# Forward decayed keys turned by VectorE and a round trip through HBM, instead of by TensorE

## The chip, the cores and the metric

The kernel runs on one core of one Trainium2 chip. The metric is the device time of one execution in microseconds, the median over runs; lower is better. The profile names the engines: PE is TensorE (matmul) and PEld its weight loads, DVE is VectorE, ACT is ScalarE, POOL is GpSimd, and SP is SyncE, which issues nearly all DMAs here.

## The reference, cut to what matters

One layer of an encoder over 1024 tokens of width 1024: an RMS norm, one input projection, two branches (bidirectional gated linear attention, and a pooling mixer), a gated merge, and a SwiGLU feed-forward. All is float32. The change touches the attention alone, 4 heads with keys of 128 and values of 256 features, once forward and once backward in time:

```python
b = jnp.cumsum(log_a, axis=3)            # decay within a chunk, per key feature
q_e = q * jnp.exp(b)
k_e = k * jnp.exp(-b)
k_d = k * jnp.exp(b_last - b)
scores = jnp.einsum('bhncd,bhnsd->bhncs', q_e, k_e)     # masked afterwards
o_intra = jnp.einsum('bhncs,bhnse->bhnce', scores, v)
kv = jnp.einsum('bhnsd,bhnse->bhnde', k_d, v)           # sums over the tokens of a chunk
# state: S_n+1 = diag(decay_n) S_n + kv_n
o_inter = jnp.einsum('bhncd,bhnde->bhnce', q_e, s_in)
```

The scores sum over key features, so they want the decayed keys with the features on partitions. The product `kv` sums over tokens, so it wants the same keys with the tokens on partitions.

## The kernel before, in words

Every float32 operand of a large product is split into a high part in TensorE's fast float32 form (a cast on ACT) and the low remainder (a subtract on VectorE or POOL); a product is three matmuls, high by high, high by low and low by high (`products`, L270). `split_to` (L199) is that cast and subtract.

The program is written out in order by hand: each engine executes its own instructions in the order in which the program lists them, and waits only for what its next instruction needs. `pump` (L161) is called after each group of three matmuls of a main stage (projections) and starts pieces of side work between them: a generator yields how many such groups pass before it goes on. `attention(h)` is such a generator. While head h is worked on, the main stage is a projection: values and then queries and keys of later heads, and for the last head the output gate `r`.

A head works on 8 chunks of 128 tokens, in two halves of 512 tokens, with d = 0 for the forward and d = 1 for the backward direction; a key tile is called by (half, d). In this order: the decays of the four (half, d), each a prefix scan on VectorE (`decay`), exponentials on ACT, and `apply_decay`, which makes the decayed keys `ke` on VectorE and the decayed queries `qe` on POOL. `transposed_keys` (L896) turns one `ke` tile token-major: four 128x128 transposes on TensorE into one bank of PSUM (`kp`), then `split_to` into a tile `kt`. The backward tiles (1,1) and (0,1) are turned before the backward scan over the chunks n = 7 down to 1. A step of a scan is `advance` (L904): three matmuls into a bank `kv`, an update of the state `st` on VectorE, and two scaled copies on ACT, one that goes to the output products (`sb` backward, `sf` forward) and one that the next step reads (`so`). During the step n = 7 the last `apply_decay`, of (1,0), is issued. After the step n = 3 the forward tile (0,0) is turned. Then come the scores of the first half (`scores`: matmuls into two banks `sc`, a masked merge on VectorE, and a cast and a subtract into `p`), a pause of six groups, and the forward loop over n = 0 to 7 (products of `p` and `v`, of `qe` and the states, into a bank `op`). After its step n = 0 the forward tile (1,0) is turned; the scores of the second half follow its step n = 1.

Work tiles of 4 KB per partition come from one ring of 39 buffers (`slot`, L97): raw weights, sums, keys, queries, values, states. A new tile is handed the buffer that has been free longest, in the program's order, and its first writer waits for that buffer's last reader. PSUM has 8 banks, 3 for the projections and 5 for the attention (`ps_g`). SP's queue carries the loads of weights (`raw`, L208), of sums (`wsum`, L597), of head outputs (`ol`, L1033), and the stores of sums and heads, each in program order; SP can be far ahead of the other engines, as it waits only for buffers and data.

Of the kernel before, what the change touches and what calls it, by code (L numbers as in the profile page):

```python
# [10 lines left out]
F32 = mybir.dt.float32  # L11
F32R = mybir.dt.float32r
# [5 lines left out]
P = 128  # L18
# [4 lines left out]
HALF = 512  # L23
HEADS = 4
# [5 lines left out]
GROUPS = 4  # L30
WINDOWS = (2, 4, 8, 16)
PAD = 8
D_FF = 2816
FT = D_FF // P
EPS = 1e-6
# [18 lines left out]
def kernel(  # L54
# [20 lines left out]
    nc = tc.nc  # L75
# [12 lines left out]
    dram = ctx.enter_context(tc.tile_pool(name="dram", bufs=1, space=bass.MemoryType.DRAM))  # L88
# [4 lines left out]
    def name(s):  # L93
        count[0] += 1
        return f"{s}_{count[0]}"

    def slot(dtype=F32, shape=(2, HALF), s="slot"):  # L97
        return slots.tile([P, *shape], dtype, tag="slot", name=name(s))

    def t2(width=HALF, dtype=F32, s="t"):  # L100
        return tmp.tile([P, width], dtype, tag="t2", name=name(s), padded_shape=[P, HALF + 2 * PAD])

# [3 lines left out]
    def vec(width, s="v"):  # L106
        return small.tile([P, width], F32, tag="vec", name=name(s), bufs=12)

    def bank(pool, s="ps"):
        return pool.tile([P, HALF], F32, tag=pool.name, name=name(s))  # L110

    def as_f32(ap):
        return ap.bitcast(F32)
# [4 lines left out]

    keepf = tmp.tile([P, HALF], F32, tag="t2", name="keepf", padded_shape=[P, HALF + 2 * PAD])
    nc.gpsimd.memset(keepf[:, :P], 1.0)  # L120
# [12 lines left out]

    edge = const.tile([P, 2, GROUPS, PAD], F32, tag="edge", name="edge")
    nc.gpsimd.memset(edge[:, :, :, :], 1.0)
    for g, w in enumerate(WINDOWS):
        for i in range(w // 2):
            nc.gpsimd.memset(edge[:, 0, g, i : i + 1], w / (i + w // 2))
        for i in range(1, w // 2):
            nc.gpsimd.memset(edge[:, 1, g, PAD - i : PAD - i + 1], w / (i + w // 2))  # L140

# [57 lines left out]
    def split_to(hi, lo, src, eng=nc.vector):  # L199
        nc.scalar.copy(hi, src)  # L200
        eng.tensor_tensor(lo, src, as_f32(hi), op=ALU.subtract)  # L201
# [392 lines left out]
    def loading(srcs, tiles):  # L594
        def loads():
            for t, src in zip(tiles, srcs):
                nc.sync.dma_start(t, src)  # L597

        yield loads, None, None
        for _ in range(2):  # L600
            yield None, None, None
# [23 lines left out]
    def unit_jobs(n):  # L625
        raw = [slot(F32, (KT, P), "fraw")[:, :, :] for _ in range(2)]
        a11, a12, a21, a22 = (t[:, 4 * j : 4 * j + 4, :].rearrange("p k c -> p (k c)") for t in raw for j in range(2))
        yield from loading(
            [w_ffn_in[:, c0 : c0 + P].rearrange("(k p) c -> p k c", p=P) for c0 in (f_order[n] * P, D_FF + f_order[n] * P)], raw
        )  # L630
# [100 lines left out]
            aside.pop(0)  # L731


    o_heads, unscaled = {}, []
    HOLD, SCORES = 5.0, 6

# [76 lines left out]
    def attention(h):  # L813


        qe, ke = {}, {}
# [48 lines left out]
        def exponentials(half, d):  # L865
            if half not in qe:
                qe[half] = slot(s="qe")
            cs, tot, e_q = zs[half, d], totals[half, d], qe[half]
            f = vec(12, "fac")
            sign = INV_NORMALIZER if d == 0 else -INV_NORMALIZER  # L870
            nc.scalar.activation(e_q[:, d, :], cs[:, :], AF.Exp, scale=sign)
            nc.scalar.activation(cs[:, :], cs[:, :], AF.Exp, scale=-sign)
            nc.scalar.activation(f[:, :8], tot[:, :], AF.Exp, scale=INV_NORMALIZER)
            fac[half, d] = f

        def apply_decay(half, d):
            if half not in ke:
                ke[half] = slot(s="ke")
            f, e_q, e_k = fac[half, d], qe[half], ke[half]
            f2 = f[:, :8].rearrange("p (n a) -> p n a", a=2)  # L880
            nc.vector.tensor_tensor(e_k[:, d, :], zs[half, d][:, :], k[:, half, :], op=ALU.mult)
            nc.gpsimd.tensor_tensor(e_q[:, d, :], e_q[:, d, :], q[:, half, :], op=ALU.mult)
            nc.gpsimd.tensor_tensor(f[:, 8:], f2[:, :, 0], f2[:, :, 1], op=ALU.mult)
# [9 lines left out]
        def chunk_of(e, n, d):  # L893
            return e[n // 4][:, d, (n % 4) * CH : (n % 4 + 1) * CH]

        def transposed_keys(half, d):  # L896
            kp = bank(ps_g, "kp")
            for i in range(4):
                nc.tensor.transpose(kp[:, i * P : (i + 1) * P], chunk_of(ke, 4 * half + i, d), ident[:, :])
            kt = slot(F32R, s="kt")  # L900
            split_to(kt[:, 0, :], kt[:, 1, :], kp[:, :])
            return kt

        def advance(old, n, d, kt, dst, ends=False):  # L904

            kv = bank(ps_g, "kv")
            products(kv[:, :DV], tokens((kt[:, 0, :], kt[:, 1, :]), n), value(n))
            new = s1((DV,), "st")[:, :]
            after = factor(n, d, "after")
            if old is None:  # L910
                nc.vector.tensor_scalar(new, kv[:, :DV], after, None, op0=ALU.mult)
            else:
                nc.vector.scalar_tensor_tensor(
                    new, kv[:, :DV], after, old[:, :], op0=ALU.mult, op1=ALU.add
                )
            following = n + 1 if d == 0 else n - 1
            nc.scalar.activation(dst, new, AF.Copy, scale=factor(following, d, "before"))
            if ends:
                return None
            old = s1((DV,), "so")  # L920
            nc.scalar.activation(old[:, :], new, AF.Copy, scale=factor(following, d, "whole"))
            return old

        def scores(half):
            sc = [bank(ps_g, "sc") for _ in range(2)]
            for d in range(2):
                for i in range(4):
                    n = 4 * half + i
                    nc.tensor.matmul(
                        sc[d][:, i * CH : (i + 1) * CH], chunk_of(ke, n, d), chunk_of(qe, n, d),  # L930
                        start=True, stop=True,
                    )
            hi, lo = (t2(dtype=F32R, s="p")[:, :] for _ in range(2))
            nc.vector.copy_predicated(sc[1][:, :], keep.rearrange("p n c -> p (n c)"), sc[0][:, :])
            split_to(hi, lo, sc[1][:, :])
            return hi, lo
# [17 lines left out]
        kts = {(1, 1): transposed_keys(1, 1)}  # L954
# [2 lines left out]
        decay(1, 0)  # L957
        yield HOLD - 2
        kts[0, 1] = transposed_keys(0, 1)
        exponentials(1, 0)  # L960
        yield 2.5
        def value(n):
# [4 lines left out]
        for n in range(NT - 1, 0, -1):  # L967
            m = n - 1
            while n not in v_tiles[h]:
                yield 0.5  # L970
            old = advance(old, n, 1, kts[n // 4, 1], sb[m // 4][:, m % 4, :], m == 0)
            if n == 7:
                apply_decay(1, 0)
            yield 1.2
            if n == 3:
                kts[0, 0] = transposed_keys(0, 0)
                yield 0.5
        p = scores(0)
        yield SCORES
# [5 lines left out]
        for n in range(NT):  # L985
            half, i = n // 4, n % 4
            op = bank(ps_g, "op")
            products(op[:, :DV], tokens(p, n), value(n), last=False)
            terms = []
            if n < NT - 1:  # L990
                terms.append((chunk_of(qe, n, 1), sb[half][:, i, :]))
            if n > 0:
                terms.append((chunk_of(qe, n, 0), sf[:, :]))
            for j, (a, b) in enumerate(terms):
                if j == len(terms) - 1 and n < NT - 1:
                    sf = s1((DV,), "sf")
                    old = advance(old, n, 0, kts[half, 0], sf[:, :], n == NT - 2)
                nc.tensor.matmul(op[:, :DV], a, b, start=False, stop=j == len(terms) - 1)
            nc.vector.tensor_copy(o[half][:, i, :], op[:, :DV])
            nc.scalar.activation(  # L1000
                op[:, DV:], op[:, :DV], AF.Square, scale=1.0 / 16.0, accum_out=ms[:, n : n + 1]
            )
            if n == 0:
                yield 0.38
                kts[1, 0] = transposed_keys(1, 0)
            if n == 1:
                yield 0.75
                q_next = scores(1)
            if n == 3:
                p = q_next  # L1010
            yield 1.02
# [236 lines left out]
    def pooled(g, u, hi, lo):  # L1248
        width = WINDOWS[g]
        n = HALF + 2 * PAD  # L1250
        for half in range(2):
# [4 lines left out]
            while 2 * step < width:  # L1256
# [6 lines left out]
                s, step = a, 2 * step  # L1263
            e = slice(PAD, 2 * PAD) if half == 0 else slice(HALF, PAD + HALF)
            nc.vector.tensor_tensor(s[:, e], s[:, e], edge[:, half, g, :], op=ALU.mult)
# [404 lines left out]

    units = [ReadyUnit(n) if n < READY else Unit(w_ffn_in, (f * P, D_FF + f * P)) for n, f in enumerate(f_order)]

# [391 lines left out]
    for at, p in enumerate(OUT_ORDER):  # L2064
# [9 lines left out]
        for i in range(CLOSE if closing else n_of):  # L2074
            n = at * n_of + i
# [57 lines left out]
```

## Time and profile before

| what | value |
|---|---|
| median of 3 runs | 1374.98 us (1374.72 to 1375.22) |
| profiled execution, first to last instruction | 1373.4 us |
| PE busy | 1361.4 us, 99% |
| PEld busy | 1132.9 us, 82% |
| DVE, ACT, POOL busy | 836.8, 647.3, 752.1 us |
| DMA | 251.97 MB, mean 183 GB/s |
| the four heads' attention | about 85 to 325 us of the span |

The profile gives the first-to-last span of the profiled execution; the time of a run lies 1.6 us above it at the median. In the rows that follow, a group of instructions is told as engine, line, operation, output<-inputs, count, busy time and mean duration in ns. In rows in order of time the first two numbers are start and duration in us; square brackets give the idle time of the engine just before, and what ended it. Rows of equal kind that stand together are merged (x4).

### The profile page before, as it was taken

To read this page: it belongs to the slowest core of one execution; us is meant where nothing else is said; L and a number is where in the kernel's file an instruction comes from. 1 tells how busy PE (TensorE), PEld (TensorE's weight loads), DVE (VectorE), ACT (ScalarE), POOL (GpSimd) and SP (SyncE) were. 2 spreads that over 40 slices of the span, in tenths; PEclk is the share of its full clock that TensorE was granted. 3 is DMA by queue.
4 is the path that set the end of the run, shared out by engine and by line. 5 is a ranking of instruction groups with operands and counts; after the bars stand their busy time and mean duration, and the time that the engine had idled before them with its cause. 6 is when DMAs were issued, how large, how long until landed. Compare 5 with 4: busy or idle time off the path is not lost. (4 is left out here: it accounts for less than half of the span.)

```text
span 1373.4 us, 17879 instructions
## 1 busy us (share of the span) xinstructions
PE 1361.4 (99%) x6310; PEld 1132.9 (82%) x6310; DVE 836.8 (61%) x1034; ACT 647.3 (47%) x1177; POOL 752.1 (55%) x557
## 2 busy tenths in 40 slices
PE   9999999999999999999999999999999999999998
PEld 7888888888888888888888888888888888888886
DVE  6974556554735777678883955655566556343375
ACT  7365666755534445554346533333333334444253
POOL 3323723222597547667764376666676667455454
PEclk9999999999999999999999999999999999999999
DMA  6321523314778569995416355555544447985451
GB/s 227 113 87 52 181 90 92 95 60 123 245 236 278 186 198 308 373 386 216 150 71 241 112 174 176 176 176 177 176 145 137 146 136 266 384 301 187 169 215 77
DMA packets 167834, 251.97 MB, mean 183 GB/s; under 512 B 11160, under 2 KB 94144, under 8 KB 167744
## 3 DMA queue, kind: packets, MB, share of 16 engines
q1 hardware_dynamic: 167600, 250.57, 53.8%
q8 instruction: 49, 0.80, 0.2%
q14 instruction: 41, 0.34, 0.1%
q10 hardware_dynamic: 144, 0.26, 0.0%
HBM read 168.74 MB, written 82.05 MB: 183 GB/s over the span
## 5 line engine op out<-in xcount | busy, mean ns | idle before, releaser
L201 POOL TENSOR_TENSOR wl<-fs,wh 128x512 fp32r<-128x512 f32 x124 | 173.1, 1400 | 163.5 <-ACT wh L200 104.0
L273 PE MATMUL ps<-gh,wh 128*128 128x512 f32 x616 | 240.5, 390 | 0.0
L273 PE MATMUL ps<-gl,wh 128*128 128x512 f32 x616 | 239.8, 389 | 0.3 <-DVE gl L1691 0.3
L273 PE MATMUL ps<-gh,wl 128*128 128x512 f32 x616 | 239.7, 389 | 0.0
L201 POOL TENSOR_TENSOR wl<-fraw,wh 128x512 fp32r<-128x512 f32 x93 | 134.0, 1442 | 75.0 <-ACT wh L200 72.4
L201 POOL TENSOR_TENSOR ol<-gor,oh 128x1024 fp32r<-128x1024 f32 (+1 forms) x42 | 101.3, 2417 | 86.0 <-ACT oh L200 71.7
L273 PE MATMUL ps<-hh,wh 128*128 128x512 f32 x356 | 145.1, 408 | 0.7 <-ACT ga L1474 0.7
L273 PE MATMUL ps<-hh,wl 128*128 128x512 f32 x356 | 139.0, 390 | 0.0
L273 PE MATMUL ps<-hl,wh 128*128 128x512 f32 x356 | 138.8, 390 | 0.0
L273 PEld LDWEIGHTS ps<-gl,wh 128*128 128x128 f32 x616 | 115.7, 188 | 24.5 <-DVE gl L1691 0.7
L273 PEld LDWEIGHTS ps<-gh,wh 128*128 128x128 f32 x616 | 115.7, 188 | 24.1 <-ACT hb L1710 0.2
L273 PEld LDWEIGHTS ps<-gh,wl 128*128 128x128 f32 x616 | 115.7, 188 | 23.9
L273 PE MATMUL ps<-oh,oh 128*128 128x512 f32 x308 | 119.8, 389 | 0.0
L273 PE MATMUL ps<-ol,oh 128*128 128x512 f32 x308 | 119.8, 389 | 0.0
L273 PE MATMUL ps<-oh,ol 128*128 128x512 f32 x308 | 119.8, 389 | 0.0
L201 POOL TENSOR_TENSOR wl<-wraw,wh 128x512 fp32r<-128x512 f32 x56 | 92.3, 1679 | 44.7 <-ACT wh L200 44.6
L201 POOL TENSOR_TENSOR wl<-raw,wh 128x512 fp32r<-128x512 f32 x34 | 47.4, 1404 | 108.3 <-ACT wh L200 71.9
L201 DVE TENSOR_TENSOR ol<-wor,oh 128x1024 fp32r<-128x1024 f32 (+1 forms) x42 | 62.8, 1506 | 68.1 <-ACT oh L200 55.5
L200 ACT CAST wh<-fs 128x512 fp32r<-128x512 f32 x124 | 76.1, 615 | 29.5 <-DVE fs L1093 28.3
L273 PEld LDWEIGHTS ps<-hh,wl 128*128 128x128 f32 x356 | 66.8, 188 | 14.4
L273 PEld LDWEIGHTS ps<-hh,wh 128*128 128x128 f32 x356 | 67.0, 188 | 13.1 <-ACT ga L1474 1.1
L273 PEld LDWEIGHTS ps<-hl,wh 128*128 128x128 f32 x356 | 67.0, 188 | 12.0
(281 smaller groups left out, 3073.4 us busy)
## 6 DMA issues: line engine op xcount, KB each, us to landing
fraw<-in_w_ffn_in_dram SPq DMA_DIRECT2D x44, 512.0 KB, 6.1
gor<-g_out SPq DMA_DIRECT2D x35, 512.0 KB, 6.1
fraw<-in_w_in_dram SPq DMA_DIRECT2D x22, 512.0 KB, 6.5
g_out<-s SPq DMA_DIRECT2D x44, 256.0 KB, 2.3
wor<-t_out SPq DMA_DIRECT2D x20, 512.0 KB, 3.7
raw<-in_w_in_dram SPq DMA_DIRECT2D x36, 256.0 KB, 5.1
g_out<-g SPq DMA_DIRECT2D x33, 256.0 KB, 2.6
x<-in_x_dram SPq DMA_DIRECT2D x16, 512.0 KB, 5.6
```

What stands on the lines that cost most here:

```text
L200: nc.scalar.copy(hi, src)
L201: eng.tensor_tensor(lo, src, as_f32(hi), op=ALU.subtract)
L273: nc.tensor.matmul(ps, a[i], b[j], start=first and n == 0, stop=last and n == 2, skip_group_check=onto)
```

## The change

The forward tiles (0,0) and (1,0) of each head are no longer turned by TensorE. VectorE transposes `ke` in blocks of 32x32 into a slot tile `kq` (`turn_keys`), four DMAs write it to a buffer in HBM, one for each group of 32 partitions, in runs of 128 elements (`put_keys`), one DMA reads the buffer back into the other half of the same tile (`get_keys`), and `split_keys` makes `kt` from it. The backward tiles stay as they were. The new steps are issued at: `turn_keys(0,0)` after the second backward tile is turned, `put_keys(0,0)` after the backward step n = 7, `turn_keys(1,0)` after n = 6, `get_keys(0,0)` after n = 5, `put_keys(1,0)` after n = 4, `split_keys(0,0)` and then `get_keys(1,0)` after n = 1, and `split_keys(1,0)` after the forward step n = 2.

```diff
+    k_out = {
+        (h, half, d): dram.tile([P, HALF], F32, name=f"k_out{h}{half}{d}")
+        for h in range(HEADS) for half in range(2) for d in range(1)
+    }
...
+        turned = {}
+        def turn_keys(half, d):
+            both = slot(s="kq")
+            nc.vector.transpose(
+                both[:, 0, :].rearrange("p (j c b) -> p c j b", j=4, b=SQ),
+                ke[half][:, d, :].rearrange("p (c j a) -> p c j a", j=4, a=SQ),
+            )
+            turned[half, d] = both
+        def put_keys(half, d):
+            to = k_out[h, half, d].rearrange("(j a) (i m) -> i a j m", a=SQ, i=4)
+            for i in range(4):
+                src = turned[half, d][i * SQ : (i + 1) * SQ, 0, :]
+                nc.sync.dma_start(to[i], src.rearrange("p (j m) -> p j m", j=4))
+        def get_keys(half, d):
+            nc.sync.dma_start(turned[half, d][:, 1, :], k_out[h, half, d])
+        def split_keys(half, d):
+            kt = slot(F32R, s="kt")
+            hi, lo = (kt[:, i, :].rearrange("p (c i b) -> p c i b", c=4, b=SQ) for i in range(2))
+            back = turned[half, d][:, 1, :].rearrange("p (i c b) -> p c i b", i=4, b=SQ)
+            split_to(hi, lo, back)
+            kts[half, d] = kt
...
         kts[0, 1] = transposed_keys(0, 1)
+        turn_keys(0, 0)
         exponentials(1, 0)
...
             if n == 7:
                 apply_decay(1, 0)
+                put_keys(0, 0)
+            elif n == 6:
+                turn_keys(1, 0)
+            elif n == 5:
+                get_keys(0, 0)
+            elif n == 4:
+                put_keys(1, 0)
+            elif n == 1:
+                split_keys(0, 0)
+                get_keys(1, 0)
             yield 1.2
             if n == 3:
-                kts[0, 0] = transposed_keys(0, 0)
                 yield 0.5
...
             if n == 0:
                 yield 0.38
-                kts[1, 0] = transposed_keys(1, 0)
...
+            if n == 2:
+                split_keys(1, 0)
```

More of the change, by code (lines that the diff above doesn't have):

```diff
@@ L32 @@
 PAD = 8
+SQ = 32
 D_FF = 2816
```

## The prediction

> **What bounds the kernel now.** I read the page first (span, busy time, chain), then the groups of lines for the operation that goes, the waits of TensorE, and the instructions in order of time of each engine, once per head.
>
> ```profile
> span 1373.4 us, 17879 instructions
> PE 1361.4 (99%) x6310; PEld 1132.9 (82%) x6310; DVE 836.8 (61%) x1034; ACT 647.3 (47%) x1177; POOL 752.1 (55%) x557
> PEclk9999999999999999999999999999999999999999
> PE ps L273 44%; ACT gh L1687 0%; DVE gl L1691 0%; DVE hb L1724 0%; DVE hb L1727 0%; ACT g L1844 0%; ACT hb L1710 0%; ACT xn L1774 0%; DVE x L1993 0%; ACT sq L2028 0%; DVE x L2043 0%; DVE g L1846 0%; POOLq L2128 0%; POOL n3rs L314 0%; ACT wh L200 0%
> ...
> PEld op L273 <- ACT p L200: 1.0, 2, 0.7
> PEld op L273 <- DVE p L201: 0.9, 2, 0.4
> ```
>
> TensorE is busy for 99% of the span at full clock and leads the chain, so one microsecond of its work is one microsecond of the kernel, if nothing makes it wait. The last two rows (weight-load waits: total, times, longest) name the weak place: the products with `p`, the masked scores of a head, already wait for ACT and VectorE in two heads. The profiled span is 1373.4 us and the median of the runs 1374.98; I put the sum on the span and add the same 1.6 us.
>
> **What the change removes.** In each of four heads two sets of four transposes (L899 for (0,0) and (1,0)) leave TensorE, with their bank of PSUM.
>
> ```profile
> L899 PE MATMUL kp<-ident,ke 128*128 128x128 f32 x64 | 9.6, 272 | 0.0
> ...
> 100.57 0.39 PE L273 MATMUL ps<-hh,wl 128*128 128x512 f32 x1
> 100.80 0.60 PE L899 MATMUL kp<-ident,ke 128*128 128x128 f32 x4
> 101.48 0.28 PE L273 MATMUL kv<-vh,kt 128*128 128x256 f32 x1
> 102.06 0.39 PE L273 MATMUL ps<-hh,wl 128*128 128x512 f32 x1
> 102.52 0.28 PE L273 MATMUL kv<-vh,kt 128*128 128x256 f32 x1
> ```
>
> Busy time overlaps, so I price a set by starts. With a set between them, the last of the three `kv` products starts 0.91 us after the `ps` product (101.48 - 100.57); without one, 0.46 (102.52 - 102.06). A set is worth 0.45 us, and the eight that go 3.6 us. That is all the change can bring, 0.26%.
>
> **What it adds on VectorE and ACT, in head 0.** The cast and the subtract of a key tile stay (now from SBUF, taken at the same price). New are two VectorE transposes of 128x512 per head: one ahead of the backward scan's first `st`, one after its second. The cast and subtract for (0,0) move from between the fifth and sixth `st` to behind the last, ahead of the score mask in VectorE's order.
>
> ```profile
> 92.31 1.23 DVE L851 TENSOR_TENSOR_SCAN z<-carry,la 128x512 f32<-128x512 bf16 x1
> 95.45 0.68 DVE L201 TENSOR_TENSOR kt<-kp,kt 128x512 fp32r<-128x512 f32 x1
> 96.05 0.47 DVE L911 TENSOR_SCALAR st<-kv,fac 128x256 f32<-128x256 f32 x1
> 99.03 0.48 DVE L913 SCALAR_TENSOR_TENSOR st<-kv,fac,so 128x256 f32<-128x256 f32 x1 [0.98 <-ACT so L921]
> 100.49 0.48 DVE L913 SCALAR_TENSOR_TENSOR st<-kv,fac,so 128x256 f32<-128x256 f32 x1 [0.98 <-ACT so L921]
> 103.28 0.57 ACT L200 CAST kt<-kp 128x512 fp32r<-128x512 f32 x1
> 103.88 0.69 DVE L201 TENSOR_TENSOR kt<-kp,kt 128x512 fp32r<-128x512 f32 x1 [1.45 <-ACT kt L200]
> 105.94 0.49 DVE L913 SCALAR_TENSOR_TENSOR st<-kv,fac,so 128x256 f32<-128x256 f32 x1 [0.97 <-ACT so L921]
> 106.34 0.69 DVE L934 COPY_PREDICATED sc<-keep,sc 128x512 f32<-128x512 uint8 x1
> 106.46 0.51 ACT L917 ACTIVATE sb<-st,fac 128x256 f32<-128x256 f32 x1 [0.56 <-DVE st L913]
> 107.68 0.69 DVE L201 TENSOR_TENSOR p<-sc,p 128x512 fp32r<-128x512 f32 x1 [0.65 <-ACT p L200]
> 110.02 0.19 PEld L273 LDWEIGHTS op<-vh,p 128*128 128x128 f32 x1
> ```
>
> No row shows a VectorE transpose. Its bounds are the subtract of 128x512 (0.68) and the scan over the same 128x512 (1.23); I take 0.68, the row with one plain pass, so a transpose moves the next instruction by 0.60 (95.45 to 96.05). At 1.23 the first ones of heads 0 and 3 and the late one of head 1 would cost 0.55 more each, and the second ones no longer fit the gap named below, 0.25 each in heads 0, 2 and 3: 2.4 us together, the far end. A gain from them is excluded, since no VectorE work goes. The Trainium skill, "VectorE: DVE Perf Modes", section "The three transpose paths", gives 311 ns for a 128x128 transpose in blocks of 32x32 (bf16); as an estimate four of these are 1.24 us, and by it the sum below would be those 2.4 us higher.
>
> The scan goes in steps of 1.46 us (99.03 to 100.49), in which VectorE idles 0.98. So the second transpose hides; the first shifts the scan: first `st` 96.65, second 98.16, the last, five steps on and without the cast in between, 105.46 (it was 105.94). From the start of the last `st` to the end of `p` it was 2.43 (105.94 to 107.68 + 0.69). With the key cast and subtract in between it is 0.52 to `sb`, 0.41 to the cast, 0.60 to the subtract, 0.61 to the mask, and 2.03 from the mask to the end of `p`: 4.17. So `p` ends at 109.63 instead of 108.37. TensorE asked for the low half of `p` at 110.02 and now comes 0.45 sooner, at 109.57. Head 0 thus keeps nearly all: -0.4 before this point, -0.45 for the second set, about **-0.8 us**. The cover of the late `p` is used up.
>
> **Head 2** begins its scan behind an idle gap that takes up the first transpose, but its slack is smaller.
>
> ```profile
> 231.10 0.48 DVE L913 SCALAR_TENSOR_TENSOR st<-kv,fac,so 128x256 f32<-128x256 f32 x1 [0.98 <-ACT so L921]
> 237.64 0.38 PE L273 MATMUL op<-vh,p 128*128 128x256 f32 x1 [0.22 <-DVE p L201]
> ```
>
> 231.10 is its fifth `st`; two steps on, the last starts at 234.02 and `p` ends at 238.2. TensorE waited for it to 237.64 before: +0.6, less 0.45 for the second set: **+0.15 us**.
>
> **Head 1, where the forecast is decided.** Two more tiles `kq` of the ring of 39 slots live through the scan. The ring hands out the buffer that came free longest ago.
>
> ```profile
> 161.66 0.48 DVE L913 SCALAR_TENSOR_TENSOR st<-kv,fac,so 128x256 f32<-128x256 f32 x1 [0.23 <-ACT so L921]
> 167.90 1.28 POOL L882 TENSOR_TENSOR qe<-qe,q 128x512 f32<-128x512 f32 x1
> 169.22 0.59 ACT L200 CAST kt<-kp 128x512 fp32r<-128x512 f32 x1 [1.69 <-POOL qe L882]
> 174.38 0.39 PE L273 MATMUL op<-vh,p 128*128 128x256 f32 x1 [0.22 <-DVE p L201]
> ```
>
> The cast for (0,0) waits for POOL's `qe` of this head, which it doesn't read: it is given the buffer of `q`, which that multiply reads last. In program order three slots are taken from the (0,1) key tile on: `sb`, `sb`, `kt`; the third gets the buffer of `q`. After the change the first three are `kq`, `sb`, `kq`: the third is the output of the second transpose, on VectorE. It would be due after the second `st`, at about 162, and POOL ends at 169.2. VectorE stands with the rest of the scan behind it: transpose 169.2 to 169.9, third `st` 169.85, the last, four steps on, 175.7, `p` ends at 179.9. TensorE loaded for its low half at 174.38: +5.5 us, or +4.7 if POOL's queue comes as much sooner as TensorE does. I take 5.1, less 0.45 for the second set. Together with head 0 that is +4.3 to +5.05, **+4.7 us** after two heads.
>
> **SP's queue and head 3.** SP issues 40 more DMAs, four puts and one get for each tile, and runs far ahead of the others: loads that it issues early now stand behind a put that waits for VectorE and a get that waits for the puts to land.
>
> ```profile
> 86.38 0.97 SPq L208 DMA_DIRECT2D raw<-in_w_in_dram  x2
> 266.24 1.44 SPq L1033 DMA_DIRECT2D ol<-o_out  x2
> 270.50 1.63 SPq L208 DMA_DIRECT2D raw<-in_w_in_dram  x2
> raw<-in_w_in_dram SPq DMA_DIRECT2D x28, 256.0 KB, 5.2
> ol<-o_out SPq DMA_DIRECT2D x6, 512.0 KB, 4.0
> 284.79 0.68 DVE L201 TENSOR_TENSOR kt<-kp,kt 128x512 fp32r<-128x512 f32 x1
> 291.41 0.61 ACT L200 CAST wh<-raw 128x512 fp32r<-128x512 f32 x1
> 300.24 0.19 PEld L273 LDWEIGHTS op<-vh,p 128*128 128x128 f32 x1
> ```
>
> In head 0 the round trip itself fits: puts from 96.8 and landed by about 101, the get by about 104, wanted at 106.4. The `raw` loads of 86.38 come behind the second get, at about 105, land near 110 and hold up an ACT cast by a microsecond that nothing on TensorE waits for: 0, at most 0.5. In heads 1 and 2 the loads behind the puts are wanted some ten microseconds later: 0. In head 3 the first put waits for the transpose behind 284.79 + 0.68, to 286.1; behind it come two `ol` loads (issued at 266.24 until now) and two `raw` (270.50), the first `raw` at about 288.6. With 1.25 MB ahead of it it lands at 293.8 (the row's 5.2) or up to 2 later, while ACT wants it at 291.41 and holds the scan's `sb` and `so` behind that cast. If the load is in time, the scan ends as in head 0 and TensorE gains both sets: -0.9. If ACT stands until 295, `p` ends at 301.9 and TensorE, due at 299.8, loses 2.1 to it; against before +1.2 net, and +2.0 near 296. I take **+0.75 us**.
>
> Sum: +4.7 + 0.15 + 0.75 = +5.6 on 1373.4, a span of 1379.0 and a time of **1380.6 us**. Its own range is 1378.5 to 1383.5: below, head 1 at 4.3 and head 3 at -0.9 (1378.5); above, the slow transpose, or head 1 at 5.05 and head 3 at 2.0 with part of it.
>
> **Rivals.** (1) No wait for the buffer in head 1 (it gets another one; the sign turns where that transpose starts later than about 163). Then its scan ends at 169.5, `p` at 173.7, no later than before, and head 1 gives -1.2: -0.8 - 1.2 + 0.15 + 0.75 = -1.1, time 1373.9, not slower. For it speaks that only one row shows the ring so short; against it, that the row shows just this buffer. (2) All is hidden, no wait is added: -3.6, 1371.4. Against it, the waits for `p` above, which a later `p` can only lengthen. (3) Head 1 is worse: TensorE stands over 4 us at the scores, since five `kv` results fill its five banks, and its clock falls.
>
> ```profile
> 1.40:4.70 3.30, 3.27 (x16) 3.27 (x17) 0.30 (x1) 0.98 (x2) 2.37 (x31) 1.00 0.80 277
> 4.70:7.20 2.50, 1.18 (x10) 0.94 (x9) 1.89 (x8) 1.15 (x5) 0.84 (x2) 1.00 0.71 197
> ```
>
> At the start of the kernel TensorE took 3.27 us for 16 transposes and then 1.18 for 10: half pace for 3.3 us, which costs some 1.5 us, so 1382. The Trainium skill, "TensorE: Matmul & The Clock Gate", Part 1, says that an idle window of about 3.4 us halves the clock until another busy one; of the trace only the start bears on it.
>
> **Chances.** The forecast 0.53, rival 1 0.27, rival 2 0.13, rival 3 0.07. A change under 0.2% (2.75 us) can't be told from none here. Slower is the forecast with rival 3: 0.60; same is rival 1: 0.27; faster is rival 2: 0.13. The range, 1372.5 to 1383.5, takes in rival 1 and leaves out rival 2 and the far end.
>
> **What would show it.** In the after profile: no L899 product in the forward sets, 32 fewer; a transpose of about 0.7 us on VectorE; in head 1 VectorE idle some 7 us before the second transpose, released by POOL `qe`, and TensorE idle before `sc` and `op` for about 5 us; in head 3 an ACT cast `wh<-raw` released by a DMA. I am wrong if that transpose starts near 162, or if the waits of `op` on `p` stay at 2 us in total.

## The result, and the profile after

The changed kernel takes **1382.22 us** (median of 4 runs, 1381.15 to 1383.42) against 1374.85 for the kernel before, run beside it: ratio **1.0053, 95% interval 1.0041 to 1.0065**. It is slower by 7.4 us; forecast were 5.6 us, 1380.6. The profiled execution spans 1381.7 us.

The first lines of the page of the changed kernel:

```profile
span 1381.7 us, 17888 instructions
PE 1363.8 (99%) x6278; PEld 1133.6 (82%) x6278; DVE 839.8 (61%) x1042; ACT 647.4 (47%) x1177; POOL 752.1 (54%) x557
```

TensorE has 32 instructions fewer (6278 after 6310), as it should, and yet more busy time (1363.8 after 1361.4): some products must have run longer. What it waits for, from the waits of TensorE of the changed kernel (total, times, longest):

```profile
PE op L274 <- ACT p L201: 3.0, 3, 1.5
PE sc L960 <- DVE st L944: 2.8, 1, 2.8
PE ps L274 <- ACT ga L1516: 1.3, 2, 0.7
PE ps L274 <- POOL wl L202: 1.2, 2, 1.0
PE op L274 <- DVE p L202: 0.7, 3, 0.2
```

To place the 8.3 us between the two spans I take five products that both kernels run, one behind each head's attention and one in the stage after, and compare their starts: the offset is the changed kernel's start less that of the kernel before, the step what each stretch adds to it. TensorE in order of time, the kernel before and then the changed one:

```profile
112.78 0.47 PE L273 MATMUL kv<-vh,kt 128*128 128x256 f32 x1
177.91 0.58 PE L273 MATMUL ps<-wh,hh 128*128 128x512 f32 x1
239.32 0.40 PE L273 MATMUL ps<-hl,wh 128*128 128x512 f32 x1
304.41 0.40 PE L273 MATMUL ps<-hh,wl 128*128 128x512 f32 x1
359.01 0.39 PE L273 MATMUL ps<-trl,wh 128*128 128x512 f32 x1
```

```profile
111.91 0.47 PE L274 MATMUL kv<-vh,kt 128*128 128x256 f32 x1
182.27 0.58 PE L274 MATMUL ps<-wh,hh 128*128 128x512 f32 x1
243.93 0.39 PE L274 MATMUL ps<-hl,wh 128*128 128x512 f32 x1
312.02 0.39 PE L274 MATMUL ps<-hh,wl 128*128 128x512 f32 x1
367.37 0.40 PE L274 MATMUL ps<-trl,wh 128*128 128x512 f32 x1
```

| behind | offset of the changed kernel, us | step | forecast of the step |
|---|---|---|---|
| head 0 | -0.9 | -0.9 | -0.8 |
| head 1 | +4.4 | +5.2 | +5.5 |
| head 2 | +4.6 | +0.3 | +0.15 |
| head 3 | +7.6 | **+3.0** | +0.75 |
| 359 us | +8.4 | **+0.7** | none |

After that point the offset stays (+8.3 at the end). The first three heads came out as forecast; head 3 and the stage behind it did not.

**Head 1.** ACT, VectorE, POOL and TensorE in order of time:

```profile
160.99 0.51 ACT L948 ACTIVATE sb<-st,fac 128x256 f32<-128x256 f32 x1 [2.13 <-DMA s_out<-wsum]
```

```profile
168.48 0.71 DVE L913 STREAM_TRANSPOSE kq<-ke 128x512 f32<-128x512 f32 x1 [6.07 <-POOL qe L887]
176.48 0.69 DVE L202 TENSOR_TENSOR kt<-kq,kt 128x512 fp32r<-128x512 f32 x1 [1.09 <-DMA s_out<-wsum]
178.43 0.69 DVE L202 TENSOR_TENSOR p<-sc,p 128x512 fp32r<-128x512 f32 x1 [0.65 <-ACT p L201]
```

```profile
167.15 1.30 POOL L887 TENSOR_TENSOR qe<-qe,q 128x512 f32<-128x512 f32 x1
```

```profile
169.61 3.78 PE L960 MATMUL sc<-qe,ke 128*128 128x128 f32 x16 [2.84 <-DVE st L944]
178.45 0.39 PE L274 MATMUL op<-vh,p 128*128 128x256 f32 x1 [0.41 <-ACT p L201]
```

The transpose reads nothing of `qe`; it stands 6.07 us until POOL has read `q` for the last time, because its output got that buffer. The scan stands with it, TensorE waits 2.84 us for bank space at the scores, and the 16 score products take 3.78 us. The 2.13 us of the first row, an `sb` that got the buffer of a `wsum` not yet stored, cost the scan nothing: the step that they delay ends at 162.41, six microseconds before the transpose can start.

**Head 3.** ACT and TensorE:

```profile
299.48 0.62 ACT L201 CAST wh<-raw 128x512 fp32r<-128x512 f32 x1 [3.04 <-DMA raw<-in_w_in_dram]
```

```profile
305.95 0.39 PE L274 MATMUL op<-vh,p 128*128 128x256 f32 x1 [1.53 <-ACT p L201]
306.68 0.39 PE L274 MATMUL op<-vh,p 128*128 128x256 f32 x1 [0.22 <-DVE p L202]
```

The raw load stands behind the stores on SP, ACT behind the load, the scan behind ACT, and TensorE behind `p`: the offset is +4.2 ahead of it (292.04 before, 296.19 now, for one `ps` product) and +6.3 at the third product with `p` (300.35 and 306.68). What the page's row of clock tenths is too coarse to show, windows of the trace do (us from to, length, TensorE busy and its instructions, granted clock, DMA share, GB/s):

```profile
164.10:167.50 3.40, 1.67 (x7) 1.00 0.46 151
304.10:307.50 3.40, 1.65 (x10) 1.00 0.92 296
239.50:242.90 3.40, 2.15 (x10) 1.00 0.45 122
167.50:174.50 7.00, 4.89 (x20) 0.51 0.51 146
307.50:311.00 3.50, 3.50 (x12) 0.51 0.48 145
```

The clock falls to half twice: at 167.5 for 7 us, and at 307.5 for 3.5 us. In the 3.4 us ahead of each fall TensorE was busy for 1.67 and 1.65; in head 2, where it was busy for 2.15, nothing fell. In head 1 the slow stretch is hidden, since TensorE still has to wait for `p` at 178.45. In head 3 it comes behind the wait, when TensorE is busy throughout: 3.5 us at half clock are 1.7 us of lost work.

Whether that fall comes is in part chance. All stretches between two changes of the clock in this trace are whole multiples of 3.41 us (160.4, 6.8, 133.1, 3.4), so the clock is changed on a grid; in the other traces the grid lies otherwise against the work. Only where a step of the grid starts between 303.2 and 304.5 does head 3 have as little work in one step (under 1.70 us) as there was ahead of the falls; that is 1.2 us of 3.4, so by this estimate about a third of the executions have the fall. The four executions took 1383.42, 1383.01, 1381.44 and 1381.15 us, but only the first left a trace, so whether the last two went without it is not shown.

### The profile page after: what moved, and what is told of

It is laid out like the page before. It is cut to its first block, busy times and chain, and to the rows that moved or that the text cites. A ratio compares the mean times of both kernels' runs of the same rounds, so it can differ in the third digit from the quotient of the medians.

```text
span 1381.7 us, 17888 instructions
## 1 busy us (share of the span) xinstructions
PE 1363.8 (99%) x6278; PEld 1133.6 (82%) x6278; DVE 839.8 (61%) x1042; ACT 647.4 (47%) x1177; POOL 752.1 (54%) x557
```

## Experiments

All ratios are to the kernel before, run beside each. The offsets are those of the table above, taken in each kernel's trace at the same five products:

| kernel | head 0 | head 1 | head 2 | head 3 | 359 us | time, us | ratio, 95% interval |
|---|---|---|---|---|---|---|---|
| changed | -0.9 | +4.4 | +4.6 | +7.6 | +8.4 | 1382.22 | 1.0053, 1.0041 to 1.0065 |
| own tile | -0.9 | -1.1 | -0.9 | -0.1 | +0.5 | 1375.95 | 1.0008, 1.0000 to 1.0017 |
| late puts | -0.6 | +4.5 | +4.8 | +3.9 | +4.6 | 1379.69 | 1.0032, 1.0020 to 1.0045 |
| both | -0.8 | -1.3 | -1.2 | -2.0 | -1.0 | 1374.19 | 0.9992, 0.9983 to 1.0001 |
| both, shared tensors | -0.9 | -1.1 | -0.9 | -1.8 | -1.9 | **1373.07** | **0.9984**, 0.9975 to 0.9993 |
| own tile, early trip | +0.3 | +0.4 | 0.0 | -0.9 | -0.3 | 1374.92 | 0.9997, 0.9989 to 1.0006 |
| no round trip | -0.7 | +4.9 | +5.1 | +4.2 | +4.1 | 1378.84 | 1.0027, 1.0018 to 1.0037 |
| warm in head 3 | -0.6 | +4.9 | +5.2 | +6.6 | +7.4 | 1381.24 | 1.0045, 1.0032 to 1.0057 |
| sets gone | -0.9 | -0.5 | -0.9 | -1.8 | -2.0 | 1372.98 | 0.9984, 0.9975 to 0.9993 |
| sets gone, late split | -0.9 | -1.5 | -1.4 | -2.3 | -2.4 | 1372.92 | 0.9983, 0.9974 to 0.9992 |
| before, shifted | -0.1 | +0.1 | +0.1 | +0.1 | +0.5 | 1375.78 | 1.0005, 0.9996 to 1.0014 |

**1. No buffer of the ring.**

```
 def turn_keys(half, d):
-    both = slot(s="kq")
+    both = las[half, d]          # log decays, dead by now
 ...                              # transpose into both, stores out of it, load back into it
```

> The turned keys lie in the tile of the log decays of the same half (dead by then), written by the transpose and overwritten by the way back, so that no buffer of the ring of slots is taken. Theory (the wait of the second transpose in head 1 for the ring's buffer, which POOL's qe reads last, and the half clock behind it cost head 1 some 5.2 us): VectorE no longer waits for POOL qe in that scan, no stretch at half clock near 167 us, head 1 gives back 5 to 6 us, and the time is about 1376 us, ratio to the kernel before 1.000 to 1.002; head 3 stays as it is, with its cast of wh waiting for a raw load. Rival (the key cast and subtract ahead of the mask are what makes p late, the buffer only takes the slack that is there): head 1 stays at +3 us or more, time 1379 or more, ratio 1.003 and up.

1375.95 us. VectorE in head 1 of this kernel:

```profile
161.87 0.70 DVE L913 STREAM_TRANSPOSE la<-ke 128x512 f32<-128x512 f32 x1
173.04 0.69 DVE L202 TENSOR_TENSOR p<-sc,p 128x512 fp32r<-128x512 f32 x1 [0.65 <-ACT p L201]
```

The second transpose starts at 161.87 instead of 168.48, `p` ends at 173.73 instead of 179.12, and head 1 goes from +5.2 to -0.2. The theory holds; the edit by itself is worth 6.3 us of time. It also lightens head 3, which I had not expected: its step falls from +3.0 to +0.8. The raw load is still late, but TensorE's wait for ACT's `p` is 0.88 us and not 1.53 (why it is shorter is not shown), and the clock stays whole there as it does in head 1. TensorE, and windows of head 1 and head 3:

```profile
299.84 0.38 PE L274 MATMUL op<-vh,p 128*128 128x256 f32 x1 [0.88 <-ACT p L201]
```

```profile
160.00:178.00 18.00, 16.42 (x91) 1.00 0.50 163
300.00:316.00 16.00, 15.77 (x95) 1.00 0.55 185
```

**2. Stores and loads back later**, behind head 3's own loads in SP's order.

```
 if n == 7:
     apply_decay(1, 0)
-    put_keys(0, 0)
 elif n == 6:
     turn_keys(1, 0)
-elif n == 5:
-    get_keys(0, 0)
+    put_keys(0, 0)
 elif n == 4:
+    get_keys(0, 0)
     put_keys(1, 0)
```

> The kernel after the change with the stores of the forward keys one step of the scan later and the loads back two steps and one step later, so that in head 3 two loads of o and two of raw weights stand ahead of the first store on SP instead of behind it. Theory (head 3 loses 4.2 us because these loads wait behind a store that waits for the transpose, so that ACT's cast of wh holds up the scan, and TensorE's clock falls in the wait): the raw loads are issued near 270 us again, no ACT wait for a DMA of raw of 3 us, no half clock near 308 us, head 3 at -0.9 instead of +4.2, time about 1377 us, ratio 1.001 to 1.003. Rival (the later split ahead of the mask, or the traffic of the round trip, is what delays head 3): p still ends near 306 us, gain under 1.5 us, time 1380 or more, ratio 1.004 and up.

1379.69 us. SP in order of time, this kernel first and then the changed one:

```profile
270.87 1.12 SPq L1074 DMA_DIRECT2D ol<-o_out  x2
275.26 1.63 SPq L209 DMA_DIRECT2D raw<-in_w_in_dram  x2
290.87 1.78 SPq L923 DMA_DIRECT2D k_out<-kq  x4
```

```profile
290.72 1.78 SPq L923 DMA_DIRECT2D k_out<-kq  x4
292.60 0.88 SPq L1075 DMA_DIRECT2D ol<-o_out  x2
293.59 1.19 SPq L209 DMA_DIRECT2D raw<-in_w_in_dram  x2
```

The same two raw loads are issued 18 us sooner, at 275.26, and ACT waits for no DMA before `wh` in this scan. Head 3's step is -0.9 instead of +3.0, and the granted clock from 300 to 316 us is 1.00. So all that head 3 lost hung on that place in SP's queue. In time the edit is worth 2.5 us (3.8 between the traces at 359 us, but the changed kernel's trace lies 1.2 above its median). The 1377 expected was too low: it took 4.2 for head 3, read between products on either side of the set at 291 us and of the loss near 357 us.

**3. Both edits.**

> Both edits together: the turned keys in the tile of the log decays, and the stores and loads back later, behind head 3's loads. Theory (the two waits are the whole loss): all four heads at -0.2 to -0.9 us, TensorE at full clock throughout, -2.9 us in all, time about 1372 us, ratio 0.9975 to 0.9985. Rival (the late p keeps most of it, or other waits appear): TensorE waits for p over 1 us in several heads, time 1374 to 1377 us, ratio 0.9995 to 1.0015.

1374.19 us, not the 1372 of the theory: 8.0 us are back, and up to head 3 the offset, -2.0, is about that of a kernel without the sets (-1.8, next). Then 1.0 us is lost near 357 us (experiment 7), and the eight sets are worth less than the theory took for them (experiment 4).

**4. What the removal alone is worth.** The key tile is cast from the decayed keys as they stand, so the transposition is left out.

```
-back = turned[half, d][:, 1, :].rearrange("p (i c b) -> p c i b", i=4, b=SQ)
+back = ke[half][:, d, :].rearrange("p (i c b) -> p c i b", i=4, b=SQ)
 ...                              # split_keys at the old places; no turn, put, get
```

> Left out: the transposition of the forward keys. The cast and subtract that make the key tile read the decayed keys as they stand, at the places where the kernel before makes them; no TensorE transposes of the forward keys, no VectorE transposes, no round trip. Theory (eight sets of four transposes at 0.45 us are worth 3.6 us, and that is the most the change could bring): time about 1371.4 us, ratio 0.9974. Rival (TensorE gives part of it back by waiting for p and st, which VectorE and ACT set): 1372.5 to 1374 us, ratio 0.998 to 0.9995.

> Left out: the transposition of the forward keys, as in the run without the sets, but the cast and subtract stand where the changed kernel has them, behind the last step of the scan and ahead of the mask. No VectorE transposes, no ring tiles, no round trip. It prices the move of the split. Theory (the move costs nothing in head 0, some 0.6 us in head 2, and up to 0.5 in heads 1 and 3): 0.5 to 1.5 us over the run with the split at its old place, time 1373.5 to 1374.5 us, ratio 0.9988 to 0.9996. Rival (the move is what the changed kernel loses by, without any buffer or queue): 1376 us or more, ratio 1.0006 and up.

With the split at the old places 1372.98 us, at the new places 1372.92: 2.1 to 2.3 us, not 3.6, and the move of the split costs nothing over all: head 2 loses the 0.6 expected by it (-0.4 against +0.2), head 1 wins 1.0 (+0.4 against -0.6). Here my theory fell in both runs. The eight sets do leave TensorE, but it waits longer for others. The waits of TensorE of the kernel with the split at its old place:

```profile
PE ps L274 <- POOL wl L202: 1.3, 2, 1.1
PE op L274 <- ACT p L201: 1.2, 2, 0.9
```

In head 1 POOL delivers `wl` at 166 us or later however early TensorE comes (the product that waits for it starts at 166.10 after 1.07 us here, at 166.77 after 0.44 in the kernel before), and behind it `p` is waited for longer. Heads 0 and 3 keep 0.9 each; head 1 loses 0.4 in this kernel and head 2 wins it back. About 2 us is all that the removal is worth in these two programs.

**5. The transposes without the round trip.** The split reads the transpose's output directly; stores and loads are left out, the ring tiles stay.

```
-back = turned[half, d][:, 1, :].rearrange("p (i c b) -> p c i b", i=4, b=SQ)
+back = turned[half, d][:, 0, :].rearrange("p (i c b) -> p c i b", i=4, b=SQ)
```

> Left out: the round trip through HBM; the transpose's output is split as it stands (its keys are turned within blocks of 32 alone). The VectorE transposes, their two tiles of the ring and the later splits stay as in the changed kernel. Theory (head 1 waits for the buffer, head 3 for loads behind the stores on SP): head 1 still loses about 5 us with VectorE's second transpose waiting for POOL qe, head 3 gains 0.5 to 0.9 us with its raw loads issued before 275 us, and the time is 1377.5 to 1379 us, ratio 1.002 to 1.003. Rival (the stores and loads themselves, their traffic or SP's time, hold up head 1): head 1 keeps its gain and the time is 1372 to 1374 us, ratio below 1.000.

> One more look at the kernel with the VectorE transposes and their ring tiles but without the round trip, for its trace. Theory of the ring: VectorE's second transpose in head 1 waits about 6 us for POOL qe although nothing is stored or loaded there; head 3's raw loads are issued before 275 us and head 3 gains. Theory of the addresses (below): without tensors for the round trip the stretch from 340 to 360 us loses nothing. Rival: no such wait in head 1 without the DMAs.

1378.84 us, and 1379.16 in the second run, from whose trace the offsets are taken. VectorE in its head 1:

```profile
168.94 0.71 DVE L913 STREAM_TRANSPOSE kq<-ke 128x512 f32<-128x512 f32 x1 [6.02 <-POOL qe L887]
```

The same wait with no DMA at all, +5.6 in head 1; and head 3 gains 0.9. The two mechanisms are apart: the ring sets head 1, the queue sets head 3.

**6. TensorE kept at work in head 3's wait.**

```
 op = bank(ps_g, "op")
+if n == 0 and h == 3:
+    for _ in range(12):
+        nc.tensor.transpose(op[:, :P], ident[:, :], ident[:, :])
 products(op[:, :DV], tokens(p, n), value(n), last=False)
```

> The changed kernel with twelve TensorE transposes of the identity put ahead of the first product with p in head 3, into a bank that the product overwrites: TensorE works where it idled for 1.5 us. Theory (the half clock of 3.4 us behind that wait costs 1.7 of head 3's 4.2 us): no slice under full clock between 300 and 316 us, the wait for p is still filled to the same end, time 1.5 to 1.9 us below the changed kernel, about 1380.5 us, ratio 1.0035 to 1.0045. Rival (the clock costs nothing, since TensorE would have to wait for the state and key tiles all the same): 1382 us, ratio 1.005; or the fall comes anyway.

TensorE of this kernel in order of time, and windows:

```profile
304.86 1.47 PE L1031 MATMUL op<-ident 128*128 128x128 f32 x12
306.57 0.39 PE L274 MATMUL op<-vh,p 128*128 128x256 f32 x1 [0.24 <-ACT p L201]
```

```profile
304.40:307.50 3.10, 2.64 (x18) 1.00 1.01 347
307.50:311.00 3.50, 3.50 (x21) 1.00 0.54 162
```

With useless work in the wait the clock stays whole from 307.5 to 311, where it was 0.51, and head 3's step is +1.4 instead of +3.0. So an execution without the fall has a head 3 that is 1.6 us shorter, close to the 1.7 of the windows; in the medians it is 1.0 (1381.24 against 1382.22, whose intervals overlap). That the useless work is what kept the clock up is not shown: in this execution the grid has bounds at 302.77, 306.18 and 309.60, which cut the wait in two, and without the twelve transposes TensorE would still have had 2.2 us and 3.0 us of work in the two steps, more than ahead of any fall.

This trace also bears out that the fall in head 1 costs nothing. There the clock was at half for 3.41 us instead of 6.83; TensorE only waited longer for `p` (1.32 us instead of 0.41), and head 1's step was +5.5, no smaller than the changed kernel's.

**7. The place of the tensors in DRAM.** All kernels with the round trip through eight tensors lose 0.6 to 1.0 us between head 3 and 359 us; those without it lose none. Two kernels were made: the version with both edits and two tensors for all heads in place of eight, and the kernel before with nothing but one 2 MB tensor and one store more:

```
-k_out = {(h, half, d): dram.tile([P, HALF], ...) for h in range(HEADS) for half in range(2) ...}
+k_out = {(half, d): dram.tile([P, HALF], ...) for half in range(2) ...}
```

```
+pad_out = dram.tile([P, 8, HALF], F32, name="pad_out")     # in the kernel before
 ...
+if h == 0: nc.sync.dma_start(pad_out[:, 0, :], ke[0][:, 0, :])
```

> The version with the turned keys in the tile of the log decays and the later stores and loads, with two DRAM tensors for the round trip that all heads share instead of eight, so that the tensors behind them lie 0.5 MB higher instead of 2 MB. If the place in DRAM sets the late loss: about 1373.2 us, ratio 0.9985 with the loss near 357 us gone or changed; if not: as with eight tensors, 1374.2 us, ratio 0.9992.

> The kernel before with one more DRAM tensor of 2 MB, into which one store of 256 KB goes in head 0 (of keys that nobody reads back), so that every DRAM tensor first used after it lies 2 MB higher, the ob_out tensors at the very addresses that they have with the round trip. All kernels with the round trip lose 0.6 to 1.0 us near 357 us, behind loads of hs that take 5.5 to 6.0 us to land instead of 4.4 to 4.7 and wait for stores of ob_out. Theory (the place of the tensors in DRAM does that): the loads take over 5.4 us, TensorE's offset to the kernel before grows by 0.6 us or more near 357 us, ratio 1.0004 to 1.0008. Rival (something else of the round trip does, such as the order of the transfers or the ACT and VectorE queues): landings as before, ratio 1.0000 to 1.0002.

The ACT cast that ends up late there, in the kernel before, the shifted one, the version with eight tensors and that with two:

```profile
352.11 1.05 ACT L707 CAST trh<-hs 128x1024 fp32r<-128x1024 f32 x1 [2.13 <-DMA hs<-f_out]
```

```profile
352.76 1.05 ACT L707 CAST trh<-hs 128x1024 fp32r<-128x1024 f32 x1 [2.71 <-DMA hs<-f_out]
```

```profile
351.31 1.05 ACT L708 CAST trh<-hs 128x1024 fp32r<-128x1024 f32 x1 [3.45 <-DMA hs<-f_out]
```

```profile
349.91 1.05 ACT L708 CAST trh<-hs 128x1024 fp32r<-128x1024 f32 x1 [1.80 <-DMA hs<-f_out]
```

With two tensors the wait is 1.80 us and the loss is gone: **1373.07 us, ratio 0.9984 (0.9975 to 0.9993)**, against 1374.19 with eight. Shifting the kernel before lengthens the wait from 2.13 to 2.71 and costs 0.4 us there in the trace, less than the 0.6 expected; its ratio, 1.0005 (0.9996 to 1.0014), can't be told from none. Both point the same way, so the place of the tensors probably has a part in it. It is not shown by itself: the intervals of the versions with eight and with two tensors overlap, and sharing a tensor also puts a head's stores behind the load back of the head before, which was not tried alone. The late load's own tensor, `f_out`, lies at the same address in all these programs; only tensors first used later moved. Why the load lands later stays open.

**8. An earlier round trip.** The first transpose and its stores right behind the decay of that half, the split back at its old place in the scan.

```
 apply_decay(0, 0)
+turn_keys(0, 0)
+put_keys(0, 0)
 decay(1, 0)
 ...
+elif n == 3: split_keys(0, 0)    # was at n == 1
```

> A version meant to be the best of the change: the turned keys in the tile of the log decays; the first transpose and its stores right behind the decay of that half, ahead of the scan; the load back after the scan's third step and the split at its old place after the fifth; the second round trip as in the changed kernel. Theory (with no buffer wait, the stores ahead of head 3's loads released some 5 us sooner, and the split out of the way of the mask, only the run without the sets bounds it): 1372.8 to 1374 us, ratio 0.998 to 0.9992. Rival (the added 0.7 us of transpose ahead of the other half's decay, or head 3's loads behind the stores, costs it): 1374.5 to 1377, ratio 0.9995 to 1.0015.

1374.92 us, no better than the kernel before, and head 0 is at +0.3. ACT in head 0 of this kernel:

```profile
97.53 0.62 ACT L201 CAST wh<-raw 128x512 fp32r<-128x512 f32 x1 [1.30 <-DMA raw<-in_w_in_dram]
98.37 0.62 ACT L201 CAST wh<-raw 128x512 fp32r<-128x512 f32 x1 [0.22 <-DMA raw<-in_w_in_dram]
98.89 0.51 ACT L948 ACTIVATE sb<-st,fac 128x256 f32<-128x256 f32 x1
```

In the changed kernel the same two casts wait for nothing:

```profile
95.25 1.13 ACT L201 CAST wh<-raw 128x512 fp32r<-128x512 f32 x2
```

Their loads, which SP issues at 70.13 in the changed kernel, stand behind the earlier stores here and are issued at 94.39; the casts come 2.3 us later and hold up the scan's first `sb` behind them. That is the mechanism of head 3, moved to head 0.

## Why the prediction was right, and where it was off

The time, 1382.2, lay in the range (the profiled execution, 1383.42, only just), and both forecast mechanisms, the ring's buffer and SP's queue, were the real ones. One step on the way was wrong and came out right by luck, and the largest miss is a term that was put at nothing.

- *Removed sets, 3.6 us.* As TensorE work, yes; as time, the run without the sets gave 2.1. The limit named as "all that the change can bring" was too high by 1.5 us, since ACT's `p` was as close to late as the forecast saw, and so was POOL's `wl`, which it did not name. Rivals 1 and 2 lean on it: rival 1, no buffer wait, is the run with the own tile, 1375.95 and not 1373.9, for its head 1 gives -0.2, not -1.2, and 0.6 is lost near 357 us; rival 2, all hidden, isn't reached even with nothing added.
- *The VectorE transpose, 0.68 us.* It took 0.70 to 0.71, as the subtract's row had it. The estimate from the Trainium skill, "VectorE: DVE Perf Modes", section "The three transpose paths", was 1.24 us; the trace does not bear that scaling out.
- *Head 0, -0.8; head 2, +0.15.* Measured -0.9 and +0.3. In head 0 `p` ended at 109.56; forecast 109.63.
- *Head 1, +5.5.* Measured +5.2. The buffer and the engine that held it (POOL `qe`) were right, but the count that led there was not. The forecast had `kq`, `sb`, `kq` taken in this order, so that the third tile, the second transpose's, got the buffer of `q`. The program takes both `sb` together, so the order is `kq`, `sb`, `sb`, `kq`, and the third is an `sb`. As built, the fourth still got the buffer of `q`, since one buffer more stood ahead of it in the ring, that of head 0's first `kq`, which the kernel before does not have. That is luck: with the count put right alone, the forecast would have set the wait on ACT, at the second `sb`, in the first step of the scan, and not on VectorE ahead of the second transpose. In size, POOL came at 168.45 instead of 169.2, and `p` ended at 179.12 instead of 179.9. The stretch from the last `st` to the end of `p` took 4.21 us (174.91 to 179.12), forecast 4.17. The 1.09 us that VectorE idles there before `kt`, put down to a store of `wsum`, are the key cast on ACT (175.84 to 176.44), which the forecast has in its sum; head 0 shows the same gap under its right name:

```profile
106.92 0.69 DVE L202 TENSOR_TENSOR kt<-kq,kt 128x512 fp32r<-128x512 f32 x1 [1.09 <-ACT kt L201]
```

- *Head 3, +0.75: the step that failed in size.* The load landed at 299.46; less the offset of 4.2 that TensorE had by then, that is 295.3 in times of before, inside the forecast's 293.8 to 295.8, and the wait it made belongs to the forecast's upper end (2.2 us for `p` less 0.9 for the two sets, +1.3). So +1.3 of the +3.0 is the mechanism as forecast, near its upper end. Missing is the clock: 1.7 us in the profiled execution, for which nothing was put in here. Rival 3 had the fall, its price (1.5 us) and its cause, a TensorE without work, but in head 1, where it did come and cost nothing.
- *A stretch without a term*, +0.7 near 357 us: loads of `hs` that land later, for a reason that stays open.

Sum of the steps: -0.9 + 5.2 + 0.3 + 3.0 + 0.7 = +8.3 in the spans; in the medians +7.4, since the profiled execution of the changed kernel took 1383.42, 1.2 above its median.

## What to carry to other kernels

Follow a new tile to the buffer that it will get, and ask who reads that buffer last: a wait of 6 us came from an engine with which the new instruction shared no data, and a dead tile of the right size as the output took it away. A store put into an in-order queue that runs ahead takes every later load down to its own time: put it behind the loads that are ready, and see which engine casts what they bring. And before the price of removed work is counted as gain, run the kernel without that work: here 2.1 of 3.6 us, which the version with both repairs and shared tensors then reached.

## What was not expected of the hardware

The clock fell without any idle stretch of 3 us: in head 3 the longest piece was 1.53 us, and TensorE had been busy for 1.65 of the 3.4 us before. The Trainium skill, "TensorE: Matmul & The Clock Gate", Part 1, speaks of an idle window of about 3.4 us; these traces agree with the length of a window but not with its being idle. On each trace's own grid of 3.41 us, start and end of the kernel left aside, TensorE was busy for 0.73 to 1.69 us in the five steps behind which the clock fell (two in the changed kernel, one each in those with late puts, without the round trip and warm in head 3), and for 1.87 us or more in every other step at full clock. About half busy was too little, 1.87 of 3.41 was enough.

And the load of `hs` that ACT waits for near 350 us took 4.4 to 4.7 us to land in the kernels whose later DRAM tensors lie where they did before or 0.5 MB higher, and 5.3 to 6.0 in those where they lie 2 MB higher.
